# Two transformer blocks on one Trainium2 core: the low gates' engine, the activation stores' queue, and the place and number of row steps in the first expert layer

## The chip, the core and the metric

The kernel runs on one core of a Trainium2 chip. The metric is the device time of one execution in microseconds (us). The engines are TensorE (PE, matmuls), VectorE (DVE), ScalarE (ACT), GpSimd (POOL) and SyncE (SP, which here only issues transfers). Each engine works through its own queue in order. Transfers are issued from the queues of SP and POOL and all share 16 DMA engines.

## What is computed

The reference runs two blocks of two layers each on 256 tokens of width 1024, with 256 context tokens beside them in the first block. What the change touches is the expert part of the first block's first layer (512 tokens). Each token has 128 chosen experts out of 16384, with a gate for each:

```
act = gelu(einsum('ted,td->te', u[ek], hk))
return einsum('te,ted->td', gk * act, v[ek])
```

`u` and `v` are tables of 16384 rows of 1024 numbers, `ek` the chosen rows of a token and `gk` their gates.

## The kernel before

**Two ways to the same sum.** In the first layer, 384 of the 512 tokens (`ND`) are computed densely: every expert for every token, with the gate zero where an expert was not chosen. The experts are 128 tiles of 128. Phase one (`phase_u`) makes, for each tile, the activations of 128 experts for 384 tokens: 24 matmuls into one PSUM bank (`proj`, L250), gelu on ACT (L1192), and a store to the array `actd` in HBM (L1196). Phase two (`phase_v`) loads the activations and gates back, multiplies them on DVE (L1488, L1489), and does 24 matmuls a tile that sum over all experts (`by_cols`). The other 128 tokens are computed row by row (`rows`, L1231): one step takes one chosen expert of every token. It gathers 128 rows of `u` and 128 rows of `v` (L1241, indirect DMAs from POOL's queue), makes the dot products on DVE (L1258), gelu and gate on ACT (L1254, L1255), and adds the weighted `v` rows on DVE (L1266). Three buffers hold `u` rows and two hold `v` rows; a `v` row asked for in step j is used in step j+1, and its buffer is the one that was freed in step j-1. In the second layer all 256 tokens are dense.

**Weights** are streamed by `Stream`: SP issues loads into six buffers (L195), ACT makes the rounded high part `whi` (L209), DVE the remainder `wlo` (L210). `take` keeps two units ahead, in three buffers.

**Gates** are made beside phase one, by a generator (`gates`, L1330) that `phase_u` calls 165 times in its first 114 tiles of the first layer (100 times in the second). For each 128 tokens it first routes (`route`, DVE work on top-16 lists, with `self.front` true), then makes 32 groups of four tokens in 35 steps: DVE compares indices into one-hots E and B (L1402), ACT multiplies E by the high part of the gate (Ah, L1396) and POOL by the low part (Al, L1397), four instructions each; two steps later PE multiplies B by Ah and Al (L1388, L1389), and ACT copies the bank to `stage` (L1418). There are two banks for this. When a 128-token group is done, `stage` goes to HBM in 16 stores on SP's queue (L1414).

**The order of a tile in phase one** is written out by hand: `take` (loads, high and low part), one or two side steps, the evacuation of gate banks, `proj`, gelu, a row step if gates are being made or all are done (L1193: both gathers, then the small ACT operations, then DVE's dot and accumulate), and the store of the activation of the tile before (L1196) on SP's queue. Activations have three buffers. In phase two the row steps that are left are spread over 120 tiles (L1526 to L1529), after the tile's matmuls; 40 of the tiles also make modulation columns on DVE (`mod_tile`).

Of the kernel before, what the change touches and what calls it, by code (L numbers as in the profile page):

```python
# [9 lines left out]
F32 = mybir.dt.float32  # L10
F32R = mybir.dt.float32r
F16 = mybir.dt.float16
# [4 lines left out]
ALU = mybir.AluOpType  # L17
# [221 lines left out]
class Build:  # L239
# [918 lines left out]
    def phase_u(self, l, p, hhi, hlo, tv, ti, N, NB):  # L1158

        tc, nc, S = self.tc, self.nc, self.S  # L1160
        with ExitStack() as es:
            u = es.enter_context(tc.tile_pool(name=f"pu{l}", bufs=1))
            pp = es.enter_context(tc.tile_pool(name=f"pup{l}", bufs=3, space=PSUM))
            pg = es.enter_context(tc.tile_pool(name=f"pug{l}", bufs=2, space=PSUM))
            pt = es.enter_context(tc.tile_pool(name=f"put{l}", bufs=1, space=PSUM))
            self.evac, self.gstores, self.front = [], [], True
            self.iota4 = u.tile([128, 128, 4], F16, name="iota4")
            nc.gpsimd.tensor_copy(self.iota4, self.iota_h.unsqueeze(2).to_broadcast([128, 128, 4]))
            side = self.gates(l, u, pg, pt, tv, ti, N, NB)
            self.fetch = None  # L1170
            if l == 0:
                nc.gpsimd.dma_start(self.xd, self.x)
            steps = (N // 128) * (15 + 35) + (15 if l == 0 else 0)
            NG = N - 128
            done = 0
            prev = None
            for i in range(128):
                S.lo_eng = nc.gpsimd if self.front and l else None
                unit = S.take(("U", l, i))
                want = (i + 1) * steps // 114  # L1180
                while done < want:
                    next(side, None)
                    done += 1
                self.flush_evac()
                self.flush_gstores(2 - l)
                ps = pp.tile([128, 512], F32, name="ps", tag="pp")
                self.proj(ps[:, :N], unit, hhi, hlo, slice(0, N))
                if l and i in self.KEPT:
                    act = self.keep[:, i - self.KEPT[0]]
                else:  # L1190
                    act = self.gp.tile([128, N], F32, name="act", tag="act", bufs=3)
                nc.scalar.activation(act, ps[:, :N], AF.Gelu)  # L1192
                if self.fetch and not (self.front and done < steps):  # L1193
                    next(self.fetch)
                if prev is not None and not (l and i - 1 in self.KEPT):
                    nc.sync.dma_start(self.actd[i - 1, :, :N], prev)  # L1196
                prev = act
                if l == 0 and i >= 125:
                    self.ahead[i] = act
                    prev = None  # L1200
                if i == 124:
                    self.flush_gstores(16)
                    for k in range(self.PRE if l else 0):
                        nc.sync.dma_start(self.slot(2 * k), self.actd[k, :, :N])
                        nc.sync.dma_start(self.slot(2 * k + 1)[:, :NG], self.gd[k, :, :NG])
                    if l == 0:
                        nc.sync.dma_start(self.early, self.gd[125:128, :, :NG].rearrange("a p t -> p a t"))
            if l:
                nc.sync.dma_start(self.actd[127, :, :N], prev)
            for _ in side:  # L1210
                pass
            S.lo_eng = None
# [18 lines left out]
    def rows(self):  # L1231


        nc, a = self.nc, self.a
        xr = self.x.rearrange("p k t -> p (k t)").rearrange("p (s d) -> p s d", d=1024)
        ub = [xr[:, i] for i in range(3)]
        vb = [xr[:, 3], self.vrow]
        dots, act, coef = (self.dots[:, i] for i in range(3))

        def get(dst, src, j):  # L1240
            nc.gpsimd.indirect_dma_start(out=dst, out_offset=None, in_=src,  # L1241
                                         in_offset=bass.IndirectOffsetOnAxis(ap=self.eidx[:, j:j + 1], axis=0))

        for j in range(2):
            get(ub[j], a["u_rows"], j)
        yield
        for j in range(128 + 2):
            self.fetched = j
            if j + 2 < 128:
                get(ub[(j + 2) % 3], a["u_rows"], j + 2)  # L1250
            if 0 <= j - 1 < 128:
                get(vb[(j - 1) % 2], a["v_rows"], j - 1)
                s, r = slice((j - 1) % 8, (j - 1) % 8 + 1), slice(j - 1, j)
                nc.scalar.activation(act[:, s], dots[:, s], AF.Gelu)  # L1254
                nc.scalar.activation(coef[:, s], act[:, s], AF.Copy, scale=self.rgate[:, r])  # L1255
            if j < 128:
                u = ub[j % 3].rearrange("p (k t) -> p k t", k=KD)
                nc.vector.scalar_tensor_tensor(u, u, 1.0, self.hrow, op0=ALU.mult, op1=ALU.mult,  # L1258
                                               accum_out=dots[:, j % 8:j % 8 + 1])
            if j >= 2:  # L1260
                v = vb[j % 2].rearrange("p (k t) -> p k t", k=KD)
                c = coef[:, (j - 2) % 8:(j - 2) % 8 + 1]
                if j == 2:
                    nc.vector.tensor_scalar_mul(self.acc, v, c)
                else:
                    nc.vector.scalar_tensor_tensor(self.acc, v, c, self.acc, op0=ALU.mult, op1=ALU.add)  # L1266
            yield
# [62 lines left out]
    def gates(self, l, u, pg, pt, tv, ti, N, NB):  # L1330
        nc = self.nc
# [10 lines left out]
        for tb in range(NB):  # L1342
# [8 lines left out]
            nc.scalar.activation(idT, tp[:, 0:2], AF.Copy)  # L1351
            g16 = u.tile([128, 128], F16, name="g16", tag="g16")
            ghi = u.tile([128, 128], F32, name="ghi", tag="ghi")
            glo = u.tile([128, 128], F32, name="glo", tag="glo")
            nc.scalar.activation(g16, tp[:, 2], AF.Copy, scale=GS)
            nc.vector.tensor_copy(ghi, g16)
            nc.vector.scalar_tensor_tensor(glo, tp[:, 2], GS, ghi, op0=ALU.mult, op1=ALU.subtract)
# [6 lines left out]
            def spread(v, g):  # L1364

                return v[:, 4 * g:4 * g + 4].unsqueeze(1).to_broadcast([128, 128, 4])
# [14 lines left out]
            for g in range(32 + 3):  # L1381
                if g == 3:
                    self.flush_gstores(16)
                if 0 <= g - 3:
                    B, Ah, Al = made.pop(g - 3)
                    ps = pg.tile([128, 4, 128], F32, name="gp", tag="gp")
                    for i in range(4):
                        nc.tensor.matmul(ps[:, i], B[:, :, i], Ah[:, i], start=True, stop=False)  # L1388
                        nc.tensor.matmul(ps[:, i], B[:, :, i], Al[:, i], start=False, stop=True)  # L1389
                    self.evac.append((stage[:, :, (g - 3) * 4:(g - 3) * 4 + 4], ps))  # L1390
                if 0 <= g - 1 < 32:
                    E, B = eq.pop(g - 1)
                    Ah, Al = rh(g - 1), rl(g - 1)
                    for i in range(4):
                        t = (g - 1) * 4 + i
                        nc.scalar.activation(Ah[:, i], E[:, :, i], AF.Copy, scale=ghi[:, t:t + 1])  # L1396
                        nc.gpsimd.tensor_scalar(Al[:, i], E[:, :, i], glo[:, t:t + 1], 1.0, op0=ALU.mult, op1=ALU.mult)  # L1397
                    made[g - 1] = (B, Ah, Al)
                if g < 32:
                    E, B = rE(g), rB(g)  # L1400
                    for v, k in ((E, 0), (B, 1)):
                        nc.vector.tensor_tensor(v, self.iota4, spread(idT[:, k], g), op=ALU.is_equal)  # L1402
                    eq[g] = (E, B)
                yield
# [25 lines left out]
    def phase_v(self, l, N, t0, hhi, hlo, tv, ti):  # L1430

        tc, nc, S = self.tc, self.nc, self.S
        with ExitStack() as es:
# [83 lines left out]
            for n in range(128):  # L1517
# [6 lines left out]
                    us = []  # L1524
                if l == 0:
                    if n == 0:  # L1526
                        left = 130 - self.fetched
                    for _ in range(min(n + 1, 120) * left // 120 - min(n, 120) * left // 120):
                        next(self.fetch, None)  # L1529
                    if n == 122:  # L1530
                        for _ in self.fetch:
                            pass
                        nc.gpsimd.dma_start(self.x, self.xd)
                elif n == 6:
                    nc.gpsimd.dma_start(cbx, a["cond"].to_broadcast([128, 2048]).rearrange("p (k t) -> p k t", t=256))
                if n == (10 if l else 1):
                    nc.scalar.activation(cb, cb, AF.Silu)
                k = self.mod_with(l, n)
# [525 lines left out]
```

## Time and profile before

| | us |
|---|---|
| median of 3 runs | 3993.63 (3992.09 to 3998.13) |
| the profiled execution | 3999.82 |
| its span, first to last instruction | 3998.0 |
| TensorE's granted clock over the span | 0.965 |

The page's busy times are sums over the whole span. The kernel's stages have different limits, so the rows below are mostly of single stretches. PE's busy time is modelled from the starts of its matmuls; a stretch in which PE is fully busy at a clock share of 1.00 is one in which no other engine held it up. "PEclk" is the share of full clock that was granted. In a row, "<-" before an engine or a transfer names what ended an idle time or a wait.

The first layer's phase one lies from 490 to 1272 us, its phase two from 1273 to 1811. The second layer's phase one lies from 2100 to 2514.

### The profile page before, as it was taken

The page shows a single profiled execution, that of the slowest core. Times are in us where ns is not written, and L with a number is a line of the kernel's source. Part 1 is how long each engine was busy: PE and PEld are TensorE (multiplying, and loading weights), DVE is VectorE, ACT ScalarE, POOL GpSimd, SP SyncE. Part 2 cuts the span into 40 slices and gives each one's busy share as a digit, 9 for nine tenths or more (in the row PEclk, how much of TensorE's full clock was granted, in tenths as well). Part 3 has the DMA queues.
Part 4 walks back from the last instruction along what each step waited for, and adds up shares of the span by engine and source line. Part 5 has one row for each costly group of instructions (what it writes and reads, how often), then busy time and mean ns, then how long its engine had stood idle before and what let it go on. Part 6 is the DMA issues. An engine that isn't in the chain of part 4 may idle for free.

```text
span 3998.0 us, 68042 instructions
## 1 busy us (share of the span) xinstructions
PE 3719.2 (93%) x25755; PEld 3537.5 (88%) x25755; DVE 2816.5 (70%) x5072; ACT 1904.6 (48%) x3480; POOL 1470.0 (37%) x1641
## 2 busy tenths in 40 slices
PE   6898997878878999998889999999999999999999
PEld 5787897878778999997889999999999699998799
DVE  7867986766767999986877565787666555665565
ACT  5323345455554444434345767554444454445444
POOL 3433318487595555532557373222100210001200
PEclk9999999989999999999999999999999899999899
DMA  5413266877869999984246687877655245554254
GB/s 212 137 64 132 98 193 231 293 237 254 273 231 335 352 343 345 344 307 140 85 148 197 199 271 213 279 266 254 212 184 168 89 148 184 175 181 150 79 173 150
DMA packets 299126, 831.91 MB, mean 208 GB/s; under 512 B 32469, under 2 KB 114389, under 8 KB 297749
## 3 DMA queue, kind: packets, MB, share of 16 engines
q1 hardware_dynamic: 238782, 619.25, 47.3%
q0 software_dynamic: 59296, 207.07, 14.9%
q8 instruction: 201, 3.29, 0.3%
q10 hardware_dynamic: 720, 1.25, 0.1%
q14 instruction: 127, 1.04, 0.1%
HBM read 760.40 MB, written 67.04 MB: 207 GB/s over the span
## 4 chain that ended last, share of the span: by engine, by line
PE 60%; DVE 7%; POOL 5%; DMA 5%; issue 3%; ACT 3%; SPq 0%; DVEq 0%; ACTq 0%; POOLq 0%
PE y L246 9%; PE y L247 9%; PE y L248 9%; PE ps L246 9%; PE ps L248 9%; PE ps L247 9%; DMA vrow<-in_v_rows,eidx 3%; DVE wlo L210 2%; POOL Al L1397 2%; POOL x L1241 1%; ACT whi L209 1%; DMA actd<-act 1%; DMA x<-in_v_rows,eidx 1%; POOL early L1397 1%; POOL wlo L210 1%
## 5 line engine op out<-in xcount | busy, mean ns | idle before, releaser
L210 DVE TENSOR_TENSOR wlo<-raw,whi 128x1024 fp32r<-128x1024 f32 x884 | 1088.7, 1235 | 605.0 <-ACT whi L209 595.3
L209 ACT ACTIVATE whi<-raw 128x1024 fp32r<-128x1024 f32 x952 | 1000.2, 1054 | 638.5 <-PE y L247 208.4
L246 PE MATMUL ps<-hhi,whi 128*128 128x256 f32 (+1 forms) x3368 | 1028.4, 305 | 11.8 <-ACT hhi L349 5.3
L248 PE MATMUL ps<-hhi,wlo 128*128 128x256 f32 (+1 forms) x3368 | 1011.3, 300 | 13.6 <-DVE wlo L210 7.9
L247 PE MATMUL ps<-hlo,whi 128*128 128x256 f32 (+1 forms) x3368 | 1010.6, 300 | 4.9 <-DVE hlo L449 4.1
L246 PEld LDWEIGHTS ps<-hhi,whi 128*128 128x128 f32 x3368 | 656.9, 195 | 43.1 <-issue 10.1
L248 PEld LDWEIGHTS ps<-hhi,wlo 128*128 128x128 f32 x3368 | 655.9, 195 | 36.2 <-DVE wlo L210 11.9
L247 PEld LDWEIGHTS ps<-hlo,whi 128*128 128x128 f32 x3368 | 656.6, 195 | 27.9 <-DVE hlo L449 8.2
L1397 POOL TENSOR_SCALAR Al<-E,glo 128x128 f16<-128x128 f16 x520 | 306.3, 606 | 291.5 <-DVE E L1402 287.8
L246 PE MATMUL y<-wh,whi 128*128 128x256 f32 (+1 forms) x1280 | 373.7, 292 | 14.0 <-ACT wh L509 14.0
L246 PE MATMUL ps<-h2hi,whi 128*128 128x384 f32 x1024 | 368.6, 360 | 9.1 <-ACT scs L1115 4.9
L247 PE MATMUL y<-wl,whi 128*128 128x256 f32 (+1 forms) x1280 | 373.5, 292 | 0.1
L248 PE MATMUL y<-wh,wlo 128*128 128x256 f32 (+1 forms) x1280 | 373.2, 292 | 0.0
L248 PE MATMUL ps<-h2hi,wlo 128*128 128x384 f32 x1024 | 360.9, 352 | 6.1 <-DVE wlo L210 5.8
L247 PE MATMUL ps<-h2lo,whi 128*128 128x384 f32 x1024 | 360.4, 352 | 0.0
L1192 ACT ACTIVATE act<-ps 128x384 f32<-128x384 f32 (+1 forms) x236 | 104.1, 441 | 330.6 <-PE ps L248 154.6
L246 PE MATMUL y<-h2hi,whi 128*128 128x384 f32 x768 | 257.1, 335 | 0.0
L247 PE MATMUL y<-h2lo,whi 128*128 128x384 f32 x768 | 256.9, 334 | 0.0
L248 PE MATMUL y<-h2hi,wlo 128*128 128x384 f32 x768 | 256.7, 334 | 0.0
L246 PEld LDWEIGHTS y<-wh,whi 128*128 128x128 f32 x1280 | 241.1, 188 | 14.5 <-ACT wh L509 14.5
L247 PEld LDWEIGHTS y<-wl,whi 128*128 128x128 f32 x1280 | 241.1, 188 | 0.6 <-DVE wl L510 0.6
L248 PEld LDWEIGHTS y<-wh,wlo 128*128 128x128 f32 x1280 | 241.1, 188 | 0.0
(447 smaller groups left out, 7690.9 us busy)
## 6 DMA issues: line engine op xcount, KB each, us to landing
raw<-in_pu SPq DMA_DIRECT2D x256, 512.0 KB
raw<-in_pv SPq DMA_DIRECT2D x256, 512.0 KB
raw<-in_ffn_gu SPq DMA_DIRECT2D x176, 512.0 KB
raw<-in_w_modt SPq DMA_DIRECT2D x96, 512.0 KB
raw<-in_w_in SPq DMA_DIRECT2D x88, 512.0 KB
raw<-in_ffn_dn SPq DMA_DIRECT2D x88, 512.0 KB
gd<-stage SPq DMA_DIRECT2D x48, 512.0 KB
actd<-act SPq DMA_DIRECT2D x125, 192.0 KB
```

Of the source, the lines that this page charges most:

```text
L209: self.nc.scalar.activation(hi[:, :w], raw, AF.Copy)
L210: (self.lo_eng or self.nc.vector).tensor_sub(lo[:, :w], raw, hi[:, :w])
L246: mm(ps, whi, xhi, start=first, stop=False, **kw)
L247: mm(ps, whi, xlo, start=False, stop=False, **kw)
L248: mm(ps, wlo, xhi, start=False, stop=last, **kw)
L1192: nc.scalar.activation(act, ps[:, :N], AF.Gelu)
L1241: nc.gpsimd.indirect_dma_start(out=dst, out_offset=None, in_=src, in_offset=bass.IndirectOffsetOnAxis(ap=self.eidx[:, j:j + 1], axis=0))
L1397: nc.gpsimd.tensor_scalar(Al[:, i], E[:, :, i], glo[:, t:t + 1], 1.0, op0=ALU.mult, op1=ALU.mult)
```

## The change

1. The low gates move from POOL (four instructions of 128x128 a step) to DVE (one instruction of 128x512 a step). It reads E with the token as the outer index, which is every fourth element, and the low gate factors, now kept as f16, repeated along the row.
2. In the first layer the store of a tile's activation is issued from POOL's queue, at the start of the next tile, in place of SP's queue after the next tile's gelu.
3. `rows` yields twice a step: after the two gathers and after the rest. In phase one the first half runs at the start of a tile, ahead of `take` and the side steps; the second half stands where the whole step stood.
4. A counter, `paid`, gives a row step to four tiles in five while gates are made, to none while `front` is true, and to each tile once all 165 side steps are done. Phase two spreads the half steps that are left over 120 tiles.

```diff
@@ phase_u @@
+            paid = 0
             for i in range(128):
+                if l == 0 and prev is not None:
+                    nc.gpsimd.dma_start(self.actd[i - 1, :, :N], prev)
+                    prev = None
+                if self.fetch:
+                    paid += 5 if done >= steps else 0 if self.front else 4
+                go = paid >= 5
+                if go:
+                    paid -= 5
+                    next(self.fetch)
                 S.lo_eng = nc.gpsimd if self.front and l else None
                 unit = S.take(("U", l, i))
...
                 nc.scalar.activation(act, ps[:, :N], AF.Gelu)
-                if self.fetch and not (self.front and done < steps):
+                if go:
                     next(self.fetch)
@@ rows @@
                 get(vb[(j - 1) % 2], a["v_rows"], j - 1)
+            yield
+            if 0 <= j - 1 < 128:
                 s, r = slice((j - 1) % 8, (j - 1) % 8 + 1), slice(j - 1, j)
@@ gates @@
-            glo = u.tile([128, 128], F32, name="glo", tag="glo")
+            glo = u.tile([128, 128], F16, name="glo", tag="glo")
...
-                        nc.gpsimd.tensor_scalar(Al[:, i], E[:, :, i], glo[:, t:t + 1], 1.0, op0=ALU.mult, op1=ALU.mult)
+                    nc.vector.tensor_mul(Al, E.rearrange("p k t -> p t k"),
+                                         glo[:, 4 * g - 4:4 * g].unsqueeze(2).to_broadcast([128, 4, 128]))
@@ phase_v @@
-                        left = 130 - self.fetched
+                        left = 2 * (130 - self.fetched)
```

## Rows read from the trace of the kernel before

**Rows 1.** The page, busy time of each engine over the span.

```profile
PE 3719.2 (93%) x25755; PEld 3537.5 (88%) x25755; DVE 2816.5 (70%) x5072; ACT 1904.6 (48%) x3480; POOL 1470.0 (37%) x1641
```

**Rows 2.** Busy time by stretch: window, us, engines (instructions), PEclk, DMA share, GB/s.

```profile
584.00:750.00 166.00, 130.20 (x809) 123.00 (x808) 104.12 (x151) 94.44 (x247) 146.37 (x173) 0.92 0.71 237
750.00:810.00 60.00, 54.66 (x294) 53.40 (x293) 44.21 (x109) 20.85 (x32) 5.36 (x5) 0.94 1.03 330
...
1041.00:1207.00 166.00, 129.10 (x809) 122.18 (x808) 104.30 (x153) 95.95 (x252) 151.74 (x173) 0.92 0.72 236
1207.00:1269.00 62.00, 52.13 (x291) 49.59 (x288) 45.67 (x52) 22.60 (x51) 34.90 (x27) 0.96 0.98 358
1300.00:1750.00 450.00, 450.00 (x2581) 450.00 (x2580) 416.80 (x698) 182.61 (x299) 251.27 (x298) 1.00 0.97 345
...
2187.00:2274.00 87.00, 87.00 (x811) 86.01 (x809) 47.30 (x73) 73.54 (x167) 33.69 (x92) 1.00 0.65 198
```

**Rows 3.** The same of L1192 (gelu) alone: its count is the stretch's tiles.

```profile
584.00:750.00 166.00, 11.21 (x23) 0.92 0.71 237
...
1041.00:1207.00 166.00, 11.56 (x24) 0.92 0.72 236
...
2187.00:2274.00 87.00, 9.96 (x26) 1.00 0.65 198
2492.00:2509.00 17.00, 2.30 (x6) 1.00 0.86 245
```

**Rows 4.** Waits from 584 to 1207 us: us in total, times, longest.

```profile
DVE acc L1266 <- DMA x<-in_v_rows,eidx: 90.6, 20, 6.5
...
DVE acc L1266 <- DMA vrow<-in_v_rows,eidx: 72.6, 16, 6.1
...
PE gp L1388 <- ACT stage L1418: 68.3, 24, 5.0
ACT act L1192 <- DMA actd<-act: 60.8, 14, 8.5
```

**Rows 5.** POOL in order of time, from 930 us: start, us, instruction.

```profile
930.07 3.73 POOL L1397 TENSOR_SCALAR early<-E,glo 128x128 f16<-128x128 f16 x4 [3.01 <-DVE early L1402]
933.95 1.90 POOL L1241 DMA_INDIRECT x<-in_u_rows,eidx  x1
936.16 1.45 POOL L1241 DMA_INDIRECT vrow<-in_v_rows,eidx  x1 [0.31 <-issue]
937.64 1.43 POOL L1397 TENSOR_SCALAR Al<-E,glo 128x128 f16<-128x128 f16 x4
```

**Rows 6.** DVE in order of time, same place.

```profile
933.75 1.23 DVE L210 TENSOR_TENSOR wlo<-raw,whi 128x1024 fp32r<-128x1024 f32 x1 [0.56 <-ACT whi L209]
934.89 0.42 DVE L1402 TENSOR_TENSOR E<-iota,idT 128x512 f16<-128x512 f16 x1
935.23 0.42 DVE L1402 TENSOR_TENSOR B<-iota,idT 128x512 f16<-128x512 f16 x1
935.56 1.22 DVE L1258 SCALAR_TENSOR_TENSOR x<-x,hrow 128x1024 f32<-128x1024 f32 x1
...
942.09 1.30 DVE L1266 SCALAR_TENSOR_TENSOR acc<-vrow,dots,acc 128x1024 f32<-128x1024 f32 x1 [5.31 <-DMA vrow<-in_v_rows,eidx]
```

**Rows 7.** ACT in order of time, same place.

```profile
933.62 1.30 ACT L1396 ACTIVATE Ah<-E,ghi 128x128 f16<-128x128 f16 x4
934.82 0.58 ACT L1418 ACTIVATE stage<-gp 128x512 f32<-128x512 f32 x1
938.02 0.49 ACT L1192 ACTIVATE act<-ps 128x384 f32<-128x384 f32 x1 [2.62 <-PE ps L248]
...
938.84 1.04 ACT L209 ACTIVATE whi<-raw 128x1024 fp32r<-128x1024 f32 x1
```

**Rows 8.** DVE's groups, 490 to 1272 us: count, busy us, mean ns, idle before.

```profile
L1277 DVE TENSOR_TENSOR cand<-tv 128x512 f32<-128x512 f32 x4 | 2.7, 686 | 0.0
```

**Rows 9.** Two lines' own view: count, ns min/median/max, first and last start.

```profile
L1478 POOL DMA_DIRECT2D ti<-actd x63: 546/551/620, 1269.0 to 1777.3; - x63
...
L1241 POOL DMA_INDIRECT x<-in_u_rows,eidx x128: 939/1170/2010, 533.1 to 1726.3; - x128
```

**Rows 10.** Busy time by stretch, phase two's fullest 20 us.

```profile
1620.00:1640.00 20.00, 20.00 (x117) 20.00 (x116) 19.33 (x34) 7.70 (x14) 11.67 (x14) 1.00 1.00 369
```

## The prediction

> **What bounds the kernel now.** I read the page's first line, then the busy time by stretch, then the waits of the stretches in which TensorE (PE) is not full, then one stretch in order of time. Over the span PE is busy 93% [rows 1], so a large change can only come from stretches where it isn't. By stretch [rows 2] PE is full in phase two of the first layer (450 of 450 us) and in phase one of the second (87 of 87). It is not full in phase one of the first layer: where gates are made PE is busy 130.2 of 166 us at a clock share of 0.92, and GpSimd (POOL) is the fullest engine, 146.4 of 166. There are three such stretches (584 to 750, 810 to 978, 1041 to 1207), the first and last of which stand in the rows. 23 and 24 tiles pass in their 166 us each [rows 3], 7.06 us a tile; all three hold 71 tiles. Phase two has the same 24 matmuls in a tile and does 2581 of them in 450 us [rows 2], so PE's own pace is 4.19. Some 71 x 2.87 = 204 us lie above it, and the question is how many of them go.
>
> Why they are there: VectorE (DVE) waits 90.6 + 72.6 us for gathered v rows [rows 4]. In order of time [rows 5, 6]: POOL makes low gates from 930.07 for 3.73 us, only then issues the u gather (933.95) and the v gather (936.16); DVE, done with the tile's other work at 936.8, stands until 942.09, and the split of the next weights, the next one-hots and then ScalarE (ACT) and PE stand behind it. The row was asked for late because POOL's queue put it behind the gates.
>
> **The change, part by part.** (1) *Low gates.* The low gate factors kept as f16 cost nothing, one small instruction per 128 tokens as before. Per gate step, four POOL instructions go (1.43 us a step undisturbed, 3.73 when they meet DVE work [rows 5]) and one DVE multiply of 128x512 comes. There is no such strided f16 product in the trace. From below: 0.42 us, the one-hot of as many f16 elements in order [rows 6]. From above: 0.69, an f32 tensor-tensor of that size [rows 8]. The new one reads every fourth element and repeats the gate, so I take 0.69, or about 0.61 from start to start, since the one-hot of 0.42 is followed after 0.34. The Trainium skill's page "VectorE: DVE Perf Modes", section "Mode 2×_1P — pack two bf16 into one 32-bit read", says that two 16-bit elements per cycle need step 1 in memory; by it the value is the upper one too, and by the lower one the gates' DVE sum below would be 0.4 us less a tile.
>
> (2) *Pace.* The loop makes 165 side steps in 114 tiles, 1.45 a tile. Counting the generator's turns by the code, row steps in phase one fall from 84 (one in each of 71 gate tiles and 13 later ones) to 69 (four in five, and the same 13). So a gate tile needs, on
>
> - DVE: weights' low part 1.14, one-hots 1.45 x (0.34 + 0.33), low gates 1.45 x 0.61, and 0.8 x (dot 1.22 + accumulate 1.30) [rows 6]: 1.14 + 0.97 + 0.88 + 2.02 = 5.0 us.
> - PE: 4.19 + 1.45 x 0.55 = 4.99, where 0.55 is a gate step's price in the second layer: 3.35 us a tile (87 over 26) with 0.88 steps against 2.83 (17 over 6) without [rows 3].
> - ACT: weights' high part 1.04, gelu with the two small operations 0.82 (the small ones in four tiles of five, so 0.75), 1.45 x (1.20 + 0.58) [rows 7]: 4.4.
>
> Three engines within 12% of each other, in queues that can't overtake, don't run at the largest sum. In a tile with two gate steps (45%), after PE's last product: gelu and small ones 0.82, high part 1.04, DVE's low part 1.14, low gates 0.61, one-hot 0.34, ACT's four high gates 1.20, first evacuation 0.58 = 5.7 us until a gate bank is free for the next tile (there are two); PE already waits so, 68.3 us [rows 4]. With one step PE's 4.74 rules. Mean 5.2. I add 0.3 for what remains of the row wait: **5.5 us**. So 71 x (7.06 - 5.5) = **-111 us**.
>
> (3) *Rows asked for first.* The v gather lands 5.9 us after its issue begins (936.16 to 942.09 [rows 5, 6]). Of the row step only the two gathers move; its small ACT and its DVE operations stay behind gelu. The v gather can now be issued as soon as the accumulate two steps earlier has freed its buffer, behind a store and a u gather. POOL issues no store now; its load of as many bytes takes 0.55, and its u gather 0.94 to 2.01, median 1.17 [rows 9]. I take 0.55 for the store, between nothing and the gather's 2.01: 0.55 + 1.17 + 5.93, or 7.7 us (6.9 to 10). DVE needs it one tile and then 1.14 + 1.85 + 1.22 later, 9.2 us. So the stall goes, with 1.5 us to spare; next to be late is the same row in a tile with one gate step or behind a slow issue, which is the 0.3 above.
>
> (4) *Stores from POOL.* SP no longer holds weight loads behind a store that waits for gelu, and gelu's wait for its buffer (60.8 us in these stretches [rows 4]) mostly goes. Behind the store on POOL stand only the gathers, which it can delay to the end of gelu of the tile before; this is in (3). Between gate stretches DMA is full at 330 GB/s and a share of 1.03 with gate stores, and after the last at 358 and 0.98 [rows 2]; the bytes there don't change, so I take only **-4 us** (bounds 0 to -15). The second layer keeps its stores on SP.
>
> (5) *Fewer rows in phase one, more in phase two.* 15 steps move: 61 instead of 46 in phase two, in half steps over 120 tiles of 4.19 us (2581 matmuls of 24 a tile in 450 us [rows 2]), 503 us. Each step moves two gathers of 0.52 MB: 15.7 MB, or 31 GB/s on top of 345 at a share of 0.97. 376 exceeds what any stretch read here moved: 369 in the fullest 20 us [rows 10]. On DVE 15 x 2.5 = 38 us come to 416.8 of 450, so 93% + 7.5% = 100%. Both covers are gone at once. What the engines can move lies between 356 (345 at 0.97, brought to 1) and 369 or more; I take 365, near the fullest slice: 376 against 365 costs 3%, **+15 us**. Bounds 0 (the fullest slice was not a limit) and +45 (DVE can't work without gaps either, a tile at 4.55). The Trainium skill's page "SBUF — State Buffer", section "A bandwidth-pool intuition that's wrong (but worth ruling out)", gives HBM to one core about 358 GB/s; rows 10 show 369, so the measurement decides; by 358 this term would be +25 and the sum 3904, within the forecast's own range.
>
> (6) *The second layer's phase one* also gets the DVE product: 0.88 x 0.61 us a tile beside 47.3 of 87 us busy, and POOL's gates go. PE is full there [rows 2], so **0** (bounds -3 to +3); the cover is DVE's 46% of idle time, and if it were gone the cost would be 64 x 0.61 = 39 us.
>
> **Sum.** -111 - 4 + 15 = -100 on the profiled execution's 3999.8 us (span 3998.0), which lies 6.2 above the median of 3993.6: about 3894 by the median.
>
> **Rivals**, all by the median.
>
> - *Everything fits* (gate tile at DVE's 5.0, nothing lost in phase two): 71 x 2.06 = 146, with (4) 150: 3844. For it: PE at full clock when it stops pausing (0.92 now). Against: the chain of two-step tiles.
> - *POOL still holds the rows*: the store at the head of the queue waits for gelu, the gathers follow, and gate tiles stay at 6.5: -40 - 4 + 15 = -29, 3965. For it: only 1.5 us to spare in (3). It decides once issue and landing exceed 9.2 us.
> - *Phase two takes it back, slower than before*: DMA and DVE both at 100% make each late load stall PE, and PE's clock falls after pauses as it does in the gate stretches. 115 us are won before, so it decides from 4.19 + 0.96 = 5.15 us a tile; at 5.3 it costs 133: 4012. For it: 376 GB/s. Against: DVE has room of two weights and three products ahead, and a row is now used three tiles after it was asked for.
> - *The gate tile doesn't gain*: POOL was only nominally late, and DVE, 104 us busy of 166 without the product [rows 2], becomes the bound with the same tile: +15, 4009. It needs a product several times dearer than the 0.69.
>
> **How the numbers follow.** Chances: forecast 0.52 (its own range 3865 to 3930), everything fits 0.17, POOL holds 0.19, phase two 0.05, no gain in the tile 0.03, gains and losses about equal 0.04. Faster by over 0.2% (8 us, about what a measurement of this kernel can tell): 0.52 + 0.17 + 0.19 = 0.88; within: 0.04; slower: 0.08. The range goes from 3840 to 3970: forecast, most of the two neighbours, and the bounds of (4) and (5).
>
> **What would show it.** Gate stretches of about 130 us in place of 166, POOL under 50% busy in them, the wait of the accumulate for rows under 50 us in all three, one DVE product of 0.6 to 0.7 us per step, clock share near 1. Phase two 540 to 560 us long instead of 537 (128 tiles of 4.19), with DMA share at 1.0 and DVE at 97% or more. Wrong would be: gate tiles above 6.2, a product over 0.8, gelu or gathers waiting on each other on POOL, phase two unchanged, or PE idle in it.

## The result, and the profile after

The changed kernel takes 3850.68 us (median of 4 runs, 3849.53 to 3858.19) against 3993.6 before: a ratio of 0.964, 95% interval 0.963 to 0.966, or 142 to 143 us less. The profiled execution took 3849.67 us with a span of 3847.7, against 3999.82 and 3998.0. Forecast were 3894 and a range from 3840 to 3970.

Where the 150 us between the two spans went, by the starts of gelu and of the matmuls in order of time:

| stretch | before, us | after, us | difference |
|---|---|---|---|
| up to the first gelu | 492.7 | 489.1 | -3.6 |
| first 22 tiles of phase one | 91.4 | 91.4 | 0 |
| three gate stretches of 23 tiles | 166.0 + 167.9 + 165.6 | 121.1 + 122.6 + 123.6 | -132.2 |
| two stretches of 12 tiles between them | 59.9 + 63.2 | 53.8 + 53.7 | -15.6 |
| last 12 tiles | 61.8 | 54.2 | -7.6 |
| last gelu to phase two's first matmul | 4.7 | 10.7 | +6.0 |
| phase two | 540.1 | 543.7 | +3.6 |
| all that follows | 2184.7 | 2183.8 | -0.9 |

A gate tile fell from 7.24 to 5.32 us (499.5 and 367.3 over 69 tiles). Sorted by the number of gate steps between one gelu and the next, the 29 tiles with two steps fell from 10.0 to 6.3 us on average, the 37 tiles with one from 5.2 to 4.6: four fifths of the 132 us lie in the two-step tiles. The page's first line answers to [rows 1]:

```profile
PE 3662.7 (95%) x25755; PEld 3492.3 (91%) x25755; DVE 2893.2 (75%) x5232; ACT 1898.9 (49%) x3480; POOL 1181.2 (31%) x1126
```

Busy time by stretch, as in [rows 2] (window, us, PE, PEld, DVE, ACT, POOL, PEclk, DMA share, GB/s): a gate stretch, one without gates, the last tiles, 50 us of phase two, and all of it:

```profile
580.00:702.00 122.00, 114.13 (x814) 110.21 (x813) 106.55 (x169) 92.90 (x238) 56.65 (x58) 1.00 0.81 281
702.00:756.00 54.00, 51.25 (x294) 50.30 (x293) 44.60 (x109) 21.43 (x35) 8.60 (x14) 1.00 1.06 345
...
1056.00:1112.00 56.00, 50.84 (x288) 49.30 (x286) 39.06 (x43) 22.86 (x48) 37.87 (x32) 1.00 0.98 354
...
1430.00:1480.00 50.00, 50.00 (x289) 50.00 (x288) 49.79 (x85) 20.25 (x36) 32.39 (x36) 1.00 1.01 385
...
1120.00:1662.00 542.00, 539.75 (x3072) 536.89 (x3073) 510.59 (x852) 218.06 (x378) 339.47 (x364) 1.00 0.96 358
```

In the gate stretch POOL fell from 146 to 57 us busy, PE's clock share rose from 0.92 to 1.00, and DVE is now at 106.6 of 122. VectorE's groups from 580 to 1056 us show what became of the waits of [rows 4] (the idle time before an instruction stands behind the bar):

```profile
L1410 DVE TENSOR_TENSOR Al<-E,glo 128x512 f16<-128x512 f16 x66 | 45.3, 687 | 0.0
...
L1279 DVE SCALAR_TENSOR_TENSOR acc<-vrow,dots,acc 128x1024 f32<-128x1024 f32 x27 | 34.6, 1281 | 1.3 <-DMA vrow<-in_v_rows,eidx 1.3
L1279 DVE SCALAR_TENSOR_TENSOR acc<-x,dots,acc 128x1024 f32<-128x1024 f32 x26 | 33.2, 1278 | 1.0 <-DMA x<-in_v_rows,eidx 1.0
```

The wait for gathered rows went from 163 to 2.3 us. The new product takes 0.687 us.

What sets a gate tile now can be read in a tile with two gate steps, ACT in order of time:

```profile
643.99 1.05 ACT L209 ACTIVATE whi<-raw 128x1024 fp32r<-128x1024 f32 x1
644.95 1.29 ACT L1409 ACTIVATE Ah<-E,ghi 128x128 f16<-128x128 f16 x4
647.33 1.31 ACT L1409 ACTIVATE Ah<-E,ghi 128x128 f16<-128x128 f16 x4 [1.09 <-DVE E L1416]
648.55 1.06 ACT L1432 ACTIVATE stage<-gp 128x512 f32<-128x512 f32 x2
649.51 0.47 ACT L1202 ACTIVATE act<-ps 128x384 f32<-128x384 f32 x1
...
654.08 0.50 ACT L1202 ACTIVATE act<-ps 128x384 f32<-128x384 f32 x1 [1.05 <-PE ps L248]
```

ACT waits 1.09 us for the first step's one-hot, evacuates both banks and reaches gelu without waiting for PE: in this tile ACT is the last. In the next, with one step, it waits for PE. A two-step tile takes 6.3 us on average (median 6.5), a one-step tile 4.6. That ACT bounds the two-step tile is read from this order; no run lightened ACT.

### The profile page after: what moved, and what is told of

The parts are those of the page before. It is cut to its first block, busy times and chain, and to the rows that moved or that the text cites. A ratio compares the mean times of both kernels' runs of the same rounds, so it can differ in the third digit from the quotient of the medians.

```text
span 3847.7 us, 67340 instructions
## 1 busy us (share of the span) xinstructions
PE 3662.7 (95%) x25755; PEld 3492.3 (91%) x25755; DVE 2893.2 (75%) x5232; ACT 1898.9 (49%) x3480; POOL 1181.2 (31%) x1126
## 4 chain that ended last, share of the span: by engine, by line
PE 74%; DVE 13%; ACT 5%; DMA 3%; issue 3%; POOL 2%; SPq 0%; DVEq 0%; ACTq 0%; POOLq 0%
PE ps L246 13%; PE ps L248 13%; PE ps L247 13%; PE y L246 9%; PE y L248 9%; PE y L247 9%; DVE wlo L210 3%; ACT whi L209 1%; DVE modt L719 1%; DMA x<-in_v_rows,eidx 1%; PE gp L1401 1%; POOL wlo L210 1%; DVE acc L1279 1%; PE gp L1402 1%; DMA raw<-in_w_modt 1%
## 5 line engine op out<-in xcount | busy, mean ns | idle before, releaser
L246 PE MATMUL ps<-h2hi,whi 128*128 128x384 f32 x1024 | 350.2, 342 | 5.9 <-ACT scs L1115 4.9
L248 PE MATMUL ps<-h2hi,wlo 128*128 128x384 f32 x1024 | 344.7, 337 | 4.3 <-DVE wlo L210 4.3
L247 PE MATMUL ps<-h2lo,whi 128*128 128x384 f32 x1024 | 343.7, 336 | 0.0
L210 POOL TENSOR_TENSOR wlo<-raw,whi 128x1024 fp32r<-128x1024 f32 x68 | 174.5, 2579 | 213.1 <-ACT whi L209 212.9
```

Source lines behind the costliest of these rows:

```text
L210: (self.lo_eng or self.nc.vector).tensor_sub(lo[:, :w], raw, hi[:, :w])
L246: mm(ps, whi, xhi, start=first, stop=False, **kw)
L247: mm(ps, whi, xlo, start=False, stop=False, **kw)
L248: mm(ps, wlo, xhi, start=False, stop=last, **kw)
```

## The experiments

Most kernels are one part of the change away from the kernel before ("only") or from the changed one; the last two also move the gate steps. Each ratio is to the kernel before as it ran beside that kernel (medians 3992 to 3996 us). A gain in us below is taken from the ratios or from the medians, which differ by up to 6 us. Stretches and waits are of the one profiled execution. Two explanations are set against each other: the *order theory* (row gathers come late because they stand behind the low gates in POOL's queue) and the *load theory* (POOL has too much to do in a gate stretch, wherever the gathers stand).

**Only the low gates.**

```diff
-            glo = u.tile([128, 128], F32, name="glo", tag="glo")
+            glo = u.tile([128, 128], F16, name="glo", tag="glo")
...
-                        nc.gpsimd.tensor_scalar(Al[:, i], E[:, :, i], glo[:, t:t + 1], 1.0, op0=ALU.mult, op1=ALU.mult)
+                    nc.vector.tensor_mul(Al, E.rearrange("p k t -> p t k"),
+                                         glo[:, 4 * g - 4:4 * g].unsqueeze(2).to_broadcast([128, 4, 128]))
```

> The kernel before with only the low gates moved to VectorE. Order theory (gate tiles were slow because the row gathers stood behind four low-gate instructions in GpSimd's queue and VectorE waited for the rows): GpSimd has nothing ahead of the gathers, gate tiles fall from 7.1 to about 5.7 us, VectorE's wait for rows from 163 to under 60 us; 3993.6 - 97 = about 3897 us. Load theory (GpSimd's own 146 busy us of 166 bounded the tile, wherever the gathers stand): the same size, so this run alone does not part them. Store theory (the gain comes from SP's queue): under 20 us, about 3980 us.

Measured: 3868.52 us, ratio 0.969 (0.967 to 0.972). Gate stretches 127, 130 and 129 us, the rest of phase one 260 us against 276 before. Nearly nine tenths of the whole gain, from this part alone. As its forecast said, this run doesn't part the two theories. The first gate stretch (columns as above), POOL at 65 of 127 us:

```profile
579.00:706.00 127.00, 114.73 (x808) 110.81 (x807) 118.22 (x183) 94.25 (x247) 65.45 (x46) 0.99 0.91 314
```

**Only the stores.**

```diff
+                if l == 0 and prev is not None:
+                    nc.gpsimd.dma_start(self.actd[i - 1, :, :N], prev)
+                    prev = None
```

> The kernel before with only the activation stores moved to GpSimd's queue. Order and load theories: gate tiles as before or a little longer (the store waits for gelu ahead of the gathers), the stretches between gates and the last tiles gain 23 us as they did in the changed kernel; about 3970 us. If those stretches were bound by their bytes: nothing, 3990 us.

Measured: 4020.77 us, ratio 1.007 (1.005 to 1.010): slower than before. The stretches without gates did gain (55.2 and 53.8 us), but the gate stretches grew to 177, 181 and 179 us. Busy time of the first one, and waits from 585 to 1200 us:

```profile
581.00:758.00 177.00, 134.52 (x808) 126.47 (x807) 106.53 (x152) 94.74 (x247) 162.20 (x195) 0.88 0.67 222
```

```profile
POOL actd L1179 <- ACT act L1195: 84.3, 22, 12.4
...
DVE acc L1269 <- DMA vrow<-in_v_rows,eidx: 75.8, 18, 6.0
```

POOL is at 162 of 177 us. A nearly full engine was given one more instruction a tile, with a wait for gelu in front of it. The forecast, a gain of some 20 us, missed: it had left open for the gate tiles only "a little longer".

**Only the rows first.**

```diff
+                go = self.fetch and not (self.front and done < steps)
+                if go:
+                    next(self.fetch)
                 S.lo_eng = nc.gpsimd if self.front and l else None
...
-                if self.fetch and not (self.front and done < steps):
+                if go:
                     next(self.fetch)
```

with the second `yield` in `rows` and the doubled `left` in `phase_v`.

> The kernel before with only the row step split, gathers at the start of a tile, still one step in each gate tile, low gates still on GpSimd. Order theory: the gathers are ahead of the tile's low gates, VectorE's wait for rows falls from 163 to under 60 us, gate tiles to 6.0 us; about 3920 us. Load theory: GpSimd still has its 146 us of work per stretch, gate tiles stay above 6.7; 3970 to 3995 us.

Measured: 3973.69 us, ratio 0.994 (0.992 to 0.996). This run and the next part the theories. VectorE's wait for rows did fall, to 11 us (8.0 and 3.4), as the order theory wants; the gate stretches only fell to 160, 164 and 159. Waits from 585 to 1180 us, then POOL's and DVE's own order at one place:

```profile
DVE E L1407 <- POOL Al L1402: 79.5, 44, 3.3
PE gp L1394 <- POOL Al L1402: 54.9, 38, 4.5
...
DVE E L1407 <- POOL early L1402: 33.1, 19, 3.3
```

```profile
668.88 5.26 POOL L1402 TENSOR_SCALAR Al<-E,glo 128x128 f16<-128x128 f16 x8
674.30 2.03 POOL L1244 DMA_INDIRECT x<-in_u_rows,eidx  x1 [0.17 <-issue]
```

```profile
670.32 0.68 DVE L1407 TENSOR_TENSOR E<-iota,idT 128x512 f16<-128x512 f16 x1 [3.29 <-POOL Al L1402]
```

Here POOL's gaps are at most 0.3 us (145 of 160 us busy in the first gate stretch), and DVE now waits for POOL to let go of the one-hot (there are two E buffers). The wait for rows was replaced by a wait for the low gates, 113 us in place of 163: the engine behind both is nearly full.

**The change without the low gates' move** (the two `gates` hunks undone).

> The changed kernel with the low gates put back on GpSimd (stores, rows first and four in five stay). Order theory: most of the gain stays, 3850.7 + 30 = about 3880 us. Load theory: GpSimd has a fifth fewer gathers and a store more per tile, its load is about as before; most of the gain goes, 3950 us or more.

Measured: 3975.91 us, ratio 0.995 (0.994 to 0.997). The other three parts together give some 19 us without it, as the load theory said. One of the three, the stores, costs time by itself while POOL is full; the other two without it were not run. The first gate stretch, with POOL at 140 of 157 us, and DVE's waits for the low gates from 585 to 1200 us:

```profile
579.00:736.00 157.00, 130.72 (x809) 122.60 (x808) 95.37 (x135) 92.96 (x235) 139.81 (x184) 0.89 0.66 220
```

```profile
DVE E L1415 <- POOL Al L1410: 92.3, 48, 3.9
...
DVE E L1415 <- POOL early L1410: 37.4, 24, 3.9
```

**The low gates on POOL, one instruction for four tokens.**

```diff
-                    nc.vector.tensor_mul(Al, E.rearrange("p k t -> p t k"),
+                    nc.gpsimd.tensor_mul(Al, E.rearrange("p k t -> p t k"),
```

> The changed kernel with the low gates on GpSimd again, but one instruction of 128x512 for four tokens in place of four. GpSimd's product of that size took 1.41 us in the kernel before (f32), four of 128x128 took 1.43 undisturbed and 2.4 to 2.9 on average. If it is the number of instructions, each of which can meet a VectorE instruction and wait for it: about 1.5 us a step, GpSimd is no longer full, most of the gain stays; about 3880 us. If it is the engine: as with four, about 3975 us.

Measured: 3903.96 us, ratio 0.977 (0.974 to 0.979); between the two forecasts: 72 us of the 125 between the run before this one and the changed kernel. POOL's groups in phase one from its first gates on, with four instructions (the run above) and with one:

```profile
L1410 POOL TENSOR_SCALAR Al<-E,glo 128x128 f16<-128x128 f16 x259 | 155.6, 614 | 1.9
L1410 POOL TENSOR_SCALAR early<-E,glo 128x128 f16<-128x128 f16 x120 | 83.8, 711 | 0.8
```

```profile
L1410 POOL TENSOR_TENSOR Al<-E,glo 128x512 f16<-128x512 f16 x64 | 72.4, 1138 | 9.1 <-DVE E L1416 8.1
...
L1410 POOL TENSOR_TENSOR early<-E,glo 128x512 f16<-128x512 f16 x30 | 33.2, 1106 | 5.8 <-DVE E L1416 5.4
```

Four cost 2.5 us a step (239.4 over 379 instructions, times four), one costs 1.1 (105.6 over 94). So more than half of what the move brought came without leaving POOL, from one instruction in place of four; it is also another operation (a tensor by a tensor in place of a tensor by one number per partition, and the factor in f16), and the run doesn't part that from the count. In the run with four, over the whole trace, the 462 low-gate instructions that lie beside DVE work for less than half of their time took 0.42 us at most; the 178 others took 1.03 us on average and 2.5 at most. So the long ones are those beside DVE work.

The rest isn't POOL's own pace alone: the one instruction lengthens VectorE's work. The first gate stretch with the product on POOL, then with no low product at all (the next run); VectorE is the third engine in a row, with as many instructions (136):

```profile
575.00:710.00 135.00, 115.55 (x808) 110.88 (x807) 111.03 (x136) 92.82 (x236) 96.62 (x90) 0.99 0.73 253
579.00:695.00 116.00, 113.66 (x812) 109.84 (x811) 87.10 (x136) 92.56 (x237) 56.53 (x58) 1.00 0.84 294
```

```profile
601.74 1.94 DVE L1416 TENSOR_TENSOR B<-iota,idT 128x512 f16<-128x512 f16 x1
```

```profile
602.33 1.06 POOL L1410 TENSOR_TENSOR Al<-E,glo 128x512 f16<-128x512 f16 x1
```

The one-hot beside POOL's product took 1.94 us, where it takes 0.42 otherwise [rows 6]. A low product on POOL added 24 us to VectorE's busy time in this stretch; VectorE's own product takes 21 (31 of 0.687).

**The change without the low product** (`made[g - 1] = (B, Ah, Ah)`, the product left out).

> The changed kernel without the low product: PE multiplies by the high gates twice, so the low gates are left out of the result. VectorE has 0.88 us less in a gate tile. If VectorE's sum or its place in the chain of a two-step tile sets the gate tile: 5.3 us falls to 4.8 or less, 3815 us. If ACT and PE set it: under 10 us, 3840 to 3850 us.

Measured: 3840.97 us, ratio 0.961 (0.959 to 0.963), 10 to 15 us less than the changed kernel. Phase one is 601.5 us in place of 620.5 and a gate tile 5.04 in place of 5.32, so the product costs 19 us there; phase two took 554.5 in this execution. VectorE's sum isn't what sets the gate tile: an estimated 0.88 us less work gave 0.28. All of it came in the two-step tiles (5.65 us in place of 6.3; one-step tiles stayed at 4.6), so there the product's place in the chain counts in part.

**The change without the stores' move.**

> The changed kernel with the activation stores back on SP's queue, after the next tile's gelu. If gelu's wait for its buffer costs time outside the gate stretches (57 to 58 us a stretch of no gates in place of 54, last tiles 56.5 to 61.8 in place of 54.2): 3855 to 3865 us. If the store's queue makes no difference once GpSimd is free: 3851 us.

Measured: 3865.04 us, ratio 0.968 (0.966 to 0.969). The two stretches without gates take 57.9 and 56.7 us in place of 53.8 and 53.7, the gate stretches 6 us more together. With POOL relieved the stores there are worth 13 to 14 us; with POOL full they cost 25 to 30.

**The change without the rows first.**

```diff
                 if go:
                     paid -= 5
-                    next(self.fetch)
```

with the second `yield` taken out again and `left` not doubled.

> The changed kernel with the row step whole again, behind gelu, four steps in five tiles. Load theory: GpSimd has little else to do, so the gathers start as soon as their buffers are free wherever they stand; within 8 us of 3850.7. Order theory: the gathers come a gelu and a store later, VectorE waits for rows again; 3870 us or more.

Measured: 3869.16 us, ratio 0.969 (0.968 to 0.971), and neither theory had it. Phase one is as fast as with it (618.2 against 620.5 us, and VectorE waits 2 us for rows): where the gathers stand in a tile is worth nothing there. Phase two takes 565.1 us in place of 543.7:

```profile
1122.00:1688.00 566.00, 551.80 (x3088) 544.31 (x3088) 513.23 (x859) 218.79 (x380) 333.47 (x364) 0.98 0.94 342
```

```profile
DVE acc L1276 <- DMA vrow<-in_v_rows,eidx: 20.6, 11, 6.8
```

With whole steps DVE waits 20.6 us for one of the two row buffers in place of 6.1. The split of the step pays in phase two.

**The change with a row step in every gate tile.**

> The changed kernel with a row step in every gate tile (84 instead of 69 in phase one). VectorE needs 5.5 us a gate tile in place of 5.0, phase two loses its 3.7 us of extra: 3855 to 3865 us. If VectorE is not what limits the gate tile: 3847 us, as phase two is again at TensorE's pace.

Measured: 3860.18 us, ratio 0.966 (0.964 to 0.968): phase one 634.8 us in place of 620.5, phase two 541.0 in place of 543.7. That is what the forecast said, but the intervals of the two kernels overlap (0.964 to 0.968 and 0.963 to 0.966): that four in five beats five in five by some 10 us is not clear of the noise.

**The change with three row steps in five gate tiles** (`else 3` for `else 4`).

> The changed kernel with a row step in three gate tiles of five: some 14 more row steps in phase two, 29 GB/s on top of its 370. If 370 to 385 GB/s is all that the transfers give and VectorE is full, phase two grows by 25 to 45 us and the total to 3870 to 3895 us. If they still give more: about 3845 us, since the gate tiles get shorter.

Measured: 3914.18 us, ratio 0.980 (0.978 to 0.982): 63 us worse than four in five. Gate stretches fell to 120 us each, but phase two grew to 621.9, by 78 us where 25 to 45 were expected:

```profile
1107.00:1730.00 623.00, 576.84 (x3088) 550.92 (x3088) 547.42 (x900) 225.56 (x408) 394.56 (x394) 0.97 0.93 335
```

```profile
PEld y L248 <- DVE wlo L210: 41.2, 61, 1.0
...
DVE acc L1279 <- DMA vrow<-in_v_rows,eidx: 25.6, 15, 3.2
DVE acc L1279 <- DMA x<-in_v_rows,eidx: 24.8, 14, 2.9
```

PE waits for DVE and DVE for gathered rows, while the transfers move less (335 GB/s) than in the changed kernel (358). So this is not a lack of bytes per second alone; once the queues wait for each other neither DVE (547 of 623) nor the transfers are full. Which of them falls behind first was not settled.

**Gate steps spread over 122 tiles, 69 row steps kept.**

```diff
-                want = (i + 1) * steps // 114
+                want = (i + 1) * steps // (114 if l else 122)
```

and 7 and 6 in place of 5 and 4 in the counter.

> The changed kernel with the first layer's gate steps spread over 122 tiles in place of 114, and six row steps in seven gate tiles, which keeps 69 in phase one. Two-step gate tiles fall from 38 to 29; one cost 6.4 us against 4.55 for one with one step and 4.5 for one with none. Nine less: 9 x (6.4 + 4.5 - 2 x 4.55) = 16 us, about 3835 us. If the last tiles' transfers set their time with or without gates: 3850 us.

Measured: 3841.64 us, ratio 0.961 (0.960 to 0.963). Phase one 609.9 us in place of 620.5, where 16 us were expected; phase two 551.3 in this execution.

**The same with 72 row steps** (10 and 9 in the counter).

> The same with nine row steps in ten gate tiles, 72 in phase one and three less in phase two. Phase two is again at TensorE's pace (minus 3 us), gate tiles have 0.05 more row steps (plus 0 to 8 us): within 6 us of the run beside it.

Measured: 3838.61 us, ratio 0.961 (0.959 to 0.963): phase one 615.5, phase two 540.8. It has the lowest median of this study, 12 us below the changed kernel's, with an interval that ends just where that one's begins (0.9627 and 0.9628). It is not told apart from the run beside it.

## Why the prediction was right or wrong

The direction and the range held; the likeliest value was 43 us too high and the result lies below the forecast's own range, next to the rival "everything fits", though not for its reasons: the gate tile is 5.3, not 5.0, and phase two was not free. Of the signs that it named, those of the gate stretches came (121 to 124 us, POOL at 46 to 48%, 2.3 us of waiting for rows, a product of 0.687 us, clock 0.99 to 1.00); phase two is 544 us long, but at a DMA share of 0.96 and with DVE at 94%, less full than forecast.

**The cause was misread.** "The row was asked for late because POOL's queue put it behind the gates" took a symptom for the cause. With the rows first alone their wait went and 22 to 24 us came; with the low gates alone 124 to 127 us. POOL's load, 146 of 166 us, stood in the paragraph before. The time was forecast in range all the same because (2) adds up the work of the other three engines, with POOL's gates gone, and hardly uses that reading. Part (3), "So the stall goes", was taken as one leg of the gain; without it phase one is as fast, and what it is worth (some 18 us) lies in phase two, where the forecast had counted only "a row is now used three tiles after it was asked for", against a rival.

**(1) Low gates.** 0.69 was taken for the product, 0.687 measured: the strided f16 product takes as long as the f32 product of that size (0.686, [rows 8]) and not the 0.42 of the f16 one-hot in order. The trace agrees with the condition of step 1 in the Trainium skill's page "VectorE: DVE Perf Modes", section "Mode 2×_1P — pack two bf16 into one 32-bit read".

**(2) Pace.** 5.5 us a gate tile was forecast, 5.32 measured. The chain of the two-step tile was right in kind (the run without the product and the spread of steps both bear on it) and too short (5.7 against 6.3); the one-step tile was too long (4.74 against 4.6), and of the allowance of 0.3 for rows little is left, with 2.3 us of waiting in all. (The price of a gate step on PE, 0.55, comes out at 0.59 from the forecast's own figures; that lengthens its one-step tile by 0.04.) The baseline, 7.06 over 71 tiles by windows, is 7.24 over 69 by gelu starts: with 5.5 that alone would have made -120, and with 5.32 it makes the -132 measured. The mis-sized terms are the baseline (9 us) and the pace (12 us).

**(4) Stores.** -4 was taken because the bytes between the gate stretches don't change. Between the gate stretches 15.6 us went, with 345 GB/s in place of 330 in the first of the two. Not all of this is the stores': with the low gates alone or the rows first alone, stores still on SP's queue, the two stretches take 112 us together in place of 123, and 107.5 in the changed kernel. The changed kernel without the stores' move takes 114.6. So the stores are worth 5 to 7 us there. The last tiles' 7.6 us were mostly given back ahead of phase two: gelu no longer waits for a buffer, but VectorE still stands behind the rows, and phase two's first products behind VectorE:

```profile
1117.75 1.28 DVE L1279 SCALAR_TENSOR_TENSOR acc<-x,dots,acc 128x1024 f32<-128x1024 f32 x1 [1.40 <-DMA x<-in_v_rows,eidx]
1118.95 0.42 DVE L1502 TENSOR_TENSOR w<-act,early 128x256 f32<-128x256 f32 x1
```

```profile
1119.67 0.52 ACT L509 ACTIVATE wh<-w 128x384 fp32r<-128x384 f32 x1 [6.96 <-DVE w L1503]
```

**(5) Phase two.** +15 was forecast, +3.6 measured in the changed kernel, and between +4 and +14 in the six kernels with 61 row steps in halves there (543.7, 546.0, 549.2, 550.3, 551.3, 554.5 us). What the runs refute is the limit of 365 GB/s: 50 us at 385, where [rows 10] had 369, at a DMA share of 1.01 and without a loss on PE. The 358 GB/s of the Trainium skill's page "SBUF — State Buffer", section "A bandwidth-pool intuition that's wrong (but worth ruling out)", equals the mean of this phase now, but is no limit of its stretches. That both covers were nearly gone at once was right: 14 more steps cost 78 us in phase two. The rival that takes everything back needed 115, and even that kernel stayed 2% below the one before.

**(6) Second layer.** 0 forecast, 410.6 and 410.7 us measured.

## What to carry to other kernels

When one engine is nearly full in the slow stretches, price its load before the order of its queue: here, taking away the visible wait alone moved it to the next thing that engine owed. Whether moving an instruction onto an engine's queue helps depends on what else is moved off it; here the same store cost 25 to 30 us or won 13. And work shifted into a stretch that is full by two measures can be nearly free up to a point and then dear (4 to 14 us for 15 row steps, 78 for the next 14), so step such a knob both ways.

## What the runs showed of the hardware

- Four f16 instructions of 128x128 on POOL took 2.5 us where one of 128x512 (a tensor by a tensor) took 1.1, beside a busy DVE. Undisturbed, four took 1.43 [rows 5].
- The one POOL product of 128x512 lengthened VectorE's work: 136 instructions took 111.0 us in a gate stretch, and as many 87.1 without a low product; a one-hot of 0.42 us took 1.94 beside it.
- Reads and writes of this core's memory reached 385 GB/s over 50 us.
- A plain store issued from POOL's queue held it for 0.54 to 0.72 us (0.55 was taken from the loads of [rows 9]).
- The profiled executions of six kernels with the same phase two differed by 11 us in it (2%), at granted clocks of 0.99 to 1.00, with DVE at 92 to 94% and DMA at 0.95 to 0.96. With one profile of each kernel, it isn't known whether the kernels or the executions differ.
